# Context matmuls of the first expert layer: four column groups at a time, in rows of four sets, with gate and up weights alternating

## The chip, the cores and the metric

The kernel runs on one core of one Trainium2 chip. The metric is the device time of one execution in microseconds (us); the median of three runs before the change is 4630.0 us. The engines are named as the profile names them: PE (TensorE, the 128x128 array) with PEld (its weight loads), DVE (VectorE), ACT (ScalarE), POOL (GpSimd) and SP (SyncE, which issues the large transfers).

## The reference

The model is a trunk block followed by two layers of a second block. Only the last step of each of the two layers matters here, the mixture of experts in which every expert chooses its rows:

```python
def expert_choice_moe(h, w_router, w_gate, w_up, w_down):
    cap = EC_FACTOR * n // N_EXPERTS          # 128 of 1024 latent rows, 32 of 256 context rows
    aff = softmax(h @ w_router)
    g, idx = top_k(swapaxes(aff, 1, 2), cap)
    xs = h[idx]
    hid = silu(xs @ w_gate[e]) * (xs @ w_up[e])      # 1024 -> 512
    y = (hid @ w_down[e]) * g                        # 512 -> 1024
    return zeros.at[idx].add(y)
...
x = x + g2 * expert_choice_moe(modulate_2(x, sh2, sc2), ...)
if not last:                                  # the first of the two layers alone
    xc = xc + cg2 * expert_choice_moe(modulate_2(xc, csh2, csc2), ...)   # the same weights
```

All inputs are float32. There are 16 experts. In the first layer each expert works on 128 latent rows and on 32 context rows with the same weights; in the second layer on the latent rows alone.

## The kernel before

`Block2.experts` (from line 998) is called once a layer. **Weights** come in pieces of 512 KB, a tile `raw` of 128x1024 float32: `moe_plan` (line 900) lists them in the order of use. An expert has twelve: four of gate (two blocks of 128 features each), four of up, and, one expert later in the list, four of down. `fetch` issues their transfers on SP into `NR` rotating tiles; `moe_bufs` (line 146) gives `NR` = 13 for the first layer and 19 (and four early ones) for the second. `cut` splits each piece into a high and a low part, `wh` = the piece rounded to the fp32r type (a cast on ACT, line 1023) and `wl` = piece - `wh` (a subtraction on DVE, on POOL for every fourth piece, line 1024), into `NS` = 6 pairs of tiles, five pieces ahead of their use. `part` hands out the next pair.

**Latent rows.** `mm3` (lines 86 to 89) makes each product of the 128 rows of three fp32r matmuls with 512 moving columns (high x high, high x low, low x high). The way up has 8 such triples for gate (into PSUM tile `pg`) and 8 for up (`pu`), the way down 8 (`py0`, `py1`).

**Context rows.** Their 32 rows are multiplied in plain float32 straight with the unsplit piece, by `groups` (line 1059): the stationary operand has 32 columns, so it takes a fourth of the array's columns, and up to four different blocks of 256 weight columns can run in the four fourths. On the way up every `mm3` triple is followed by one *set* of two such matmuls: gate columns in fourths 0 and 1, up columns in fourths 2 and 3 of `pcx`. On the way down every two triples are followed by a set of four matmuls into `pcy`. In the trace each of these matmuls is two instructions. A `raw` tile can be loaded again only when its subtraction and its context matmuls are done.

**Order.** The instructions of this stage stand on each engine in the order of the program (`manual_schedule`). For expert e it is: way up of e; transposes of the next expert's gathered rows (line 1052); way down of e-1; transposes of the hidden rows (lines 1097 and 1102). After the way up, `th`, `hid` (lines 1080 to 1083) and their context twins `thc`, `upc`, `hcx` (lines 1086 to 1091) turn `pg`, `pu` and `pcx` into hidden rows; after the way down, `y` (line 1145) and `yc` (line 1125) weight the rows, and POOL's indirect DMAs add them to the rows they came from (lines 1146 and 1127). POOL also issues the gathers (line 1038). The last expert of the first layer has its four context sets of the way down ahead of its triples, four in a row.

Of the kernel before, what the change touches and what calls it, by code (L numbers as in the profile page):

```python
# [24 lines left out]
def bc_rows(ap, n, extra=()):  # L25
    """DRAM vector read by every partition."""
    return bass.AP(tensor=ap.tensor, offset=ap.offset, ap=[[0, P]] + list(extra) + [[1, n]])


class Base:  # L30
# [23 lines left out]
    def rsqrt(self, pool, ss, n, scale, eps, out=None):  # L54
        """(ss * scale + eps) ** -0.5 of a [128, n] tile, by Newton's iteration."""
# [6 lines left out]
        # every step turns the sign  # L62
# [28 lines left out]
    # adaptive modulation -------------------------------------------------  # L91
    def ada_new(self, pool, pre, w_ap, bcol_ap, brow_ap, cc_ap, gates):
        """A modulation to be worked out by chunks; gates: {chunk: DRAM rows [2, 512]}."""
# [18 lines left out]
    def ada_steps(self, m, ap, pp, chunks, nk=2, bufs=3, pb=1):  # L112
        """One chunk a step."""
# [29 lines left out]
class Block2(Base):  # L143
    NE = 16
    moe_early = (0, 4)
    moe_bufs = ((13, 6, 5), (19, 6, 5))
# [7 lines left out]
    def mods2(self, l, ap, pp, bufs=3):  # L154
        """The modulation of a layer, in steps: rows of shifts, 1 + scales and gates.
        Every fourth of the columns goes through its own fourth of the array."""
# [32 lines left out]
    def mod_row(self, pool, l, w, i, n=1, name="mr", q=None, **kw):  # L189
        """n modulation rows from the i-th on every partition."""  # L190
        t = pool.tile([P, n, 1024], F32, name=name, **kw)
        (q or self.nc.sync).dma_start(t, bass.AP(tensor=self.mrow.tensor, offset=self.mrow[w, l, 1024 * i:].offset, ap=[[0, P], [1, 1024 * n]]))
        return t

    def norm(self, srcs, A, B, sp, pp, sink, rows=None, between=None, xbufs=2, copy=None):
        """srcs: list of (dram [n,1024] or SBUF [128,T,1024], first tile, tiles, which); sink(k, tok0, n, f32 tile).
        between: run after the rows are scaled; copy: engine of each scaled copy of SBUF rows."""
# [39 lines left out]
    # ---------------------------------------------------------------------  # L237
    def layer(self, l, xin, cin, xmid, cmid, hn, hnc, ready=False, crows=None):
        """xmid, cmid: the rows after this layer; hn, hnc: room for modulated rows;
        ready: its modulation is worked out; crows: the context's modulated rows, if they are. the experts are chosen."""  # L240
# [13 lines left out]
    def mixers(self, l, last, lp, xin, cin, crows):  # L254
# [27 lines left out]
        # ---- the input projection, by tiles of tokens  # L282
        with self.pool(f"w{l}") as wp, self.pool(f"wps{l}", space=PSUM) as pp:
# [15 lines left out]
            def weights(c0, cn):  # L299
                """A step splits a piece; the second parts go where the pieces split before were loaded."""  # L300
# [19 lines left out]
            # rows are scaled two tiles ahead of their products, and transposed one ahead  # L320
# [40 lines left out]
        # ---- what attention keeps  # L361
        hp = s_mix.enter_context(self.pool(f"hd{l}"))
        tps = s_mix.enter_context(self.pool(f"tps{l}", space=PSUM))
        # the rotated shared part of the keys
# [24 lines left out]
        def prep(h, S):  # L389
            """The operands of one head, in steps."""  # L390
# [72 lines left out]
        # ---- attention, one head's operands ahead  # L463
        hb = s_mix.enter_context(self.pool(f"hb{l}"))
        sets.append(head_set(hb))
        with self.pool(f"at{l}") as ap, self.pool(f"atps{l}", space=PSUM) as pp:
# [4 lines left out]
            def scores(u):  # L471
                """Unnormalised probabilities of 128 queries."""
# [84 lines left out]
    def rope2(self, dst, g, tmp):  # L557
        """dst [128, 8, 64] <- rotated g; they may be the same."""
# [10 lines left out]
    def ctx_rows(self, pool):  # L569
        """The context's rows as the first layer's input projection takes them."""  # L570
# [8 lines left out]
    def rows_in(self, x, ab, wp, fast=False):  # L579
        """The norm and the modulation of one tile of tokens."""  # L580
# [9 lines left out]
    def turn_in(self, x, wp, pp):  # L590
        """Features on partitions, as two parts."""
# [9 lines left out]
    def project_in(self, t, only_kv, h, fin, wp, pp, W, cqh, cql, ckh, ckl, kr, sskr, f, u2, gv, ssv, qln, kvln):  # L601
        """One tile of tokens: the projection, and what follows it row by row; returns the last step, fin is the last tile's."""
# [49 lines left out]
    def spatial(self, l, last, TQ, f, u2, gv, ssv, sgun, bsg):  # L652
        """Spatial gating and Fourier mixing."""
        nc, ins = self.nc, self.ins
        with self.pool(f"g{l}", side="right") as cp, self.pool(f"gps{l}", space=PSUM) as pp:
            def piece(k, o, n):
                """Room for n tokens from o of the k-th features, and the way to their place."""
                t = cp.tile([P, 512], F32, name="cat", bufs=2)
                return t, lambda: nc.sync.dma_start(self.catd[k * P:k * P + P, o:o + n], t[:, :n])
# [14 lines left out]
            # Fourier: the tokens  # L674
# [30 lines left out]
            # the gate  # L705
# [7 lines left out]
            # Fourier: the features  # L713
# [45 lines left out]
    def project(self, l, last, xin, cin, xmid, cmid, hn, hnc, ep):  # L759
        """The output projection, the rows' second norm, and the choice of every expert's rows.  # L760
        Returns the steps of the choice that are left."""
# [5 lines left out]
        with self.pool(f"r{l}", side="right") as rp, self.pool(f"rps{l}", space=PSUM) as pp:  # L767
            with self.pool(f"o{l}") as op_:
                # all the weights are on their way before there is room for their parts
# [19 lines left out]
                def turn(U):  # L789
                    """The router's view of a tile, and its affinities with those of the tiles before it."""  # L790
# [13 lines left out]
                def cat(c):  # L804
                    """The features of a tile."""
# [4 lines left out]
                def router(mr):  # L810
                    """The router's weights with the norm's scales, and what its shifts add."""
# [90 lines left out]
    def moe_plan(self, l):  # L902
        ins, plan = self.ins, []
        wg, wu, wd = (ins[n][l] for n in ("w_gate_2", "w_up_2", "w_down_2"))
        for e in range(self.NE + 1):
            if e < self.NE:
                for w in (wg, wu):
                    v = w[e].rearrange("(k p) f -> p k f", p=P)
                    plan += [v[:, k:k + 2, :] for k in range(0, 8, 2)]
# [5 lines left out]
    def route(self, rp, pp, U, af, o, tag, bufs=2):  # L915
        """Affinities of two tiles of tokens, experts on partitions from o."""
# [29 lines left out]
    def choose(self, w, T, cap, rp, pp, ep, af, tag, bufs=2):  # L946
        """The cap tokens of largest affinity of every expert, and their affinities.
        Many tokens go in two halves, sorted beside each other: of the i-th of one and the i-th last of the other
        the larger one is among the cap largest of both."""
# [48 lines left out]
    def experts(self, l, last, xmid, cmid, hn, hnc, ep, af):  # L998
        """Every expert's rows, weighted and gated, added to the rows they came from."""
        nc, ins, idx, gt = self.nc, self.ins, self.idx, self.gt  # L1000
        NE = self.NE
        with self.pool(f"x{l}") as xp, self.pool(f"xps{l}", space=PSUM) as pp, self.tc.manual_schedule():
            # the weights in the order of their use, split some pieces ahead of it
# [55 lines left out]
            def groups(out, xc, w, j0, n, start, stop):  # L1059
                """Columns of w by fourths of the array; n of them from group j0."""  # L1060
                for g in range(n):
                    nc.tensor.matmul(out[32 * (j0 + g):32 * (j0 + g) + 32, :], xc, w[:, 256 * g:256 * g + 256],  # L1062
                                     start=start, stop=stop, tile_position=(0, 32 * (j0 + g)))

            def up(U):
# [4 lines left out]
                for mi, dst in enumerate((pg, pu)):  # L1070
                    for k0 in range(0, 8, 2):
                        w = part()
                        for j in range(2):
                            k = k0 + j
                            self.mm3(dst, xh[:, k], xl[:, k], w[0][:, j], w[1][:, j], k == 0, k == 7)
                            if not last:
                                c = slice(32 * (U["e"] % 4), 32 * (U["e"] % 4) + 32)
                                groups(pcx, U["xc"][:, k, c], w[2][:, j], 2 * mi, 2, k == 0, k == 7)
# [28 lines left out]
            def down(U):  # L1107
# [9 lines left out]
                def ctx(k, w):  # L1117
                    if not last:
                        groups(pcy, U["hct"][:, k], w[2].rearrange("p a b -> p (a b)"), 0, 4, k == 0, k == 3)
# [10 lines left out]
                if e == NE - 1 and not last:  # L1130
                    w = [part() for _ in range(4)]
                    for k in range(4):
                        ctx(k, w[k])
# [3 lines left out]
                else:  # L1137
                    for k in range(4):
                        w = part()
                        main(k, w)  # L1140
                        ctx(k, w)
# [21 lines left out]
            # rows are gathered two experts ahead; an expert's way down comes after the next one's way up  # L1163
# [1061 lines left out]
```

## Time and profile before

| | us |
|---|---|
| median of three runs | 4630.0 |
| lowest and highest | 4618.5, 4631.8 |
| span of the profiled execution | 4613.0 |
| of it: first layer's experts, from the first gate matmul to the last way down | about 3016 to 3561 |
| of it: second layer's experts, from the first gate matmul to the last row addition | about 4264 to 4603 |

| engine | busy us | share of the span |
|---|---|---|
| PE | 4229.6 | 92% |
| PEld | 3189.4 | 69% |
| DVE | 2803.5 | 61% |
| ACT | 1835.0 | 40% |
| POOL | 1057.6 | 23% |

The span runs from the first to the last instruction of one execution; the run's time has some us around it. [...] A matmul's recorded duration includes the pipeline behind it, so what one costs in a stream is the distance between two starts, not its duration.

### The profile page before, as it was taken

How to read it: one execution, taken by the hardware profiler on the slowest of the kernel's cores; microseconds unless marked ns; L12 is line 12 of the kernel's file. 1: busy time of each engine (PE TensorE's matmuls, PEld its weight loads, DVE VectorE, ACT ScalarE, POOL GpSimd, SP SyncE). 2: the span in 40 equal slices, each digit the busy share in tenths (PEclk: the TensorE clock that was granted, in tenths of full speed). 3: DMA queues.
4: the chain of work that ended last, by engine and by line, in shares of the span. 5: the costliest groups of instructions: out<-in, count | busy, mean ns of one | idle time of the engine just before them, and what ended most of it. 6: DMA issues, size and time to landing. Idle time of an engine off the chain costs nothing. (4 is left out here: it accounts for less than half of the span.)

```text
span 4613.0 us, 70037 instructions
## 1 busy us (share of the span) xinstructions
PE 4229.6 (92%) x27212; PEld 3189.4 (69%) x27212; DVE 2803.5 (61%) x5419; ACT 1835.0 (40%) x3590; POOL 1057.6 (23%) x863
## 2 busy tenths in 40 slices
PE   7998999999799999999897999889998889995988
PEld 6874567777667888889786777544444767774776
DVE  5365557677686544445655665655555656656888
ACT  4233234444433211212344664144443436641665
POOL 1000012222131201100211212433342202224564
PEclk9999989899999999999898999899999889997999
DMA  6226635555562322220302013467776110135996
GB/s 230 68 87 200 206 102 127 148 124 126 106 204 90 127 86 92 92 79 27 122 19 77 13 46 122 147 202 227 216 222 190 67 57 18 53 107 198 317 349 213
DMA packets 433204, 611.92 MB, mean 133 GB/s; under 512 B 93888, under 2 KB 259920, under 8 KB 431976
## 3 DMA queue, kind: packets, MB, share of 16 engines
q1 hardware_dynamic: 403800, 527.74, 35.8%
q0 software_dynamic: 29072, 79.70, 6.6%
q8 instruction: 214, 3.51, 0.3%
q14 instruction: 118, 0.97, 0.1%
HBM read 510.29 MB, written 97.05 MB: 132 GB/s over the span
## 5 line engine op out<-in xcount | busy, mean ns | idle before, releaser
L1024 DVE TENSOR_TENSOR wl<-raw,wh 128x1024 fp32r<-128x1024 f32 x284 | 402.6, 1464 | 129.3 <-ACT wh L1023 127.2
L1023 ACT CAST wh<-raw 128x1024 fp32r<-128x1024 f32 x384 | 390.0, 1052 | 184.3 <-PE pg L89 107.2
L1024 POOL TENSOR_TENSOR wl<-raw,wh 128x1024 fp32r<-128x1024 f32 x100 | 257.6, 2582 | 420.1 <-ACT wh L1023 382.2
L87 PE MATMUL pu<-z,uh 128*128 128x256 f32 x1024 | 293.7, 287 | 4.6 <-ACT uh L77 4.6
L89 PE MATMUL pu<-z,ul 128*128 128x256 f32 x1024 | 291.1, 284 | 2.3 <-DVE ul L78 2.3
L88 PE MATMUL pu<-hl,uh 128*128 128x256 f32 x1024 | 291.0, 284 | 0.0
L2057 DVE TENSOR_TENSOR x<-x,pd 128x512 f32<-128x512 f32 x256 | 174.3, 686 | 128.2 <-PE pd L89 128.2
L87 PE MATMUL gps<-wh,hh 128*128 128x512 f32 (+2 forms) x656 | 225.5, 344 | 18.1 <-ACT hh L77 13.1
L2029 POOL TENSOR_TENSOR raw<-raw,g 128x1024 f32<-128x1024 f32 x32 | 82.1, 2580 | 638.5 <-DMA raw<-w_mlp_down 455.3
L89 PE MATMUL gps<-wh,hl 128*128 128x512 f32 (+2 forms) x656 | 222.4, 340 | 1.2 <-POOL hl L1356 1.0
L87 PEld LDWEIGHTS pu<-z,uh 128*128 128x128 f32 x1024 | 197.6, 193 | 14.8 <-issue 5.3
L87 PE MATMUL pd<-dh,ah 128*128 128x512 f32 x512 | 200.1, 391 | 2.2 <-DVE x L2057 2.0
L88 PE MATMUL pd<-dl,ah 128*128 128x512 f32 x512 | 199.6, 390 | 0.0
L89 PE MATMUL pd<-dh,al 128*128 128x512 f32 x512 | 199.5, 390 | 0.0
L89 PEld LDWEIGHTS pu<-z,ul 128*128 128x128 f32 x1024 | 197.4, 193 | 2.6 <-DVE ul L78 2.6
L88 PEld LDWEIGHTS pu<-hl,uh 128*128 128x128 f32 x1024 | 197.6, 193 | 0.1
L1062 PE MATMUL pcx<-raw,xc 128*32 128x256 f32 x1024 | 160.4, 392 | 0.0
L77 ACT CAST wh<-raw 128x512 fp32r<-128x512 f32 (+1 forms) x120 | 73.5, 614 | 203.2 <-PE gp L88 85.7
L87 PEld LDWEIGHTS gps<-wh,hh 128*128 128x128 f32 x656 | 130.8, 200 | 32.2 <-ACT hh L77 14.3
L77 ACT CAST dh<-raw 128x1024 fp32r<-128x1024 f32 x32 | 32.2, 1048 | 282.3 <-PE pd L89 276.2
L89 PEld LDWEIGHTS gps<-wh,hl 128*128 128x128 f32 x656 | 130.7, 200 | 15.0 <-POOL hl L1356 1.5
L2046 DVE TENSOR_TENSOR r<-r 128x512 f32<-128x512 f32 x64 | 54.1, 845 | 142.2 <-ACT ah L2045 142.2
(676 smaller groups left out, 12226.7 us busy)
## 6 DMA issues: line engine op xcount, KB each, us to landing
araw<-w_ada SPq DMA_DIRECT2D x144, 512.0 KB
raw<-w_gate SPq DMA_DIRECT2D x128, 512.0 KB
raw<-w_up SPq DMA_DIRECT2D x128, 512.0 KB
raw<-w_down SPq DMA_DIRECT2D x128, 512.0 KB
raw<-w_in SPq DMA_DIRECT2D x100, 256.0 KB
raw<-w_mlp_up SPq DMA_DIRECT2D x32, 512.0 KB
raw<-w_mlp_down SPq DMA_DIRECT2D x32, 512.0 KB
x<-x SPq DMA_DIRECT2D x24, 512.0 KB
```

Of the source, the lines that this page charges most:

```text
L77: nc.scalar.copy(hi, src)
L87: mm(ps, lh, rh, start=start, stop=False)
L88: mm(ps, lh, rl, start=False, stop=False)
L89: mm(ps, ll, rh, start=False, stop=stop)
L1023: nc.scalar.copy(h, raw)
L1024: (nc.gpsimd if ahead or i % 4 == 3 else nc.vector).tensor_tensor(lo, raw, asf(h), op=OP.subtract)
L1062: nc.tensor.matmul(out[32 * (j0 + g):32 * (j0 + g) + 32, :], xc, w[:, 256 * g:256 * g + 256], start=start, stop=stop, tile_position=(0, 32 ...
L2029: nc.gpsimd.tensor_tensor(raw2, raw2, g2, op=OP.mult)
L2046: nc.vector.tensor_tensor(r, r, r, op=OP.mult)
L2057: nc.vector.tensor_tensor(x[:, t, s], x[:, t, s], p, op=OP.add)
```

## The change

Four edits, all in `moe_plan`, `moe_bufs` and `experts`. The plan lists gate and up pieces by turns (gate 0, up 0, gate 1, up 1, ...), in both layers. The way up takes one piece of each at a time: two triples into `pg`, two into `pu`. In the first layer its context matmuls are kept back until two such pairs of pieces are through, and then run as four sets in a row, each set of four matmuls (gate columns in fourths 0 and 1, up columns in 2 and 3 at the same time); this happens twice an expert. On the way down the four context sets come in a row after all triples. `NR` of the first layer is 18 instead of 13. The full diff also takes out comments and docstrings; nothing else differs.

```diff
-    moe_bufs = ((13, 6, 5), (19, 6, 5))
+    moe_bufs = ((18, 6, 5), (19, 6, 5))
...
-                for w in (wg, wu):
-                    v = w[e].rearrange("(k p) f -> p k f", p=P)
-                    plan += [v[:, k:k + 2, :] for k in range(0, 8, 2)]
+                vs = [w[e].rearrange("(k p) f -> p k f", p=P) for w in (wg, wu)]
+                plan += [v[:, k:k + 2, :] for k in range(0, 8, 2) for v in vs]
...
-            def groups(out, xc, w, j0, n, start, stop):
-                for g in range(n):
-                    nc.tensor.matmul(out[32 * (j0 + g):32 * (j0 + g) + 32, :], xc, w[:, 256 * g:256 * g + 256],
-                                     start=start, stop=stop, tile_position=(0, 32 * (j0 + g)))
+            def groups(out, sets, start=True, stop=True):
+                for i, (xc, ws) in enumerate(sets):
+                    for g in range(4):
+                        nc.tensor.matmul(out[32 * g:32 * g + 32, :], xc, ws[g], start=start and i == 0, stop=stop and i == len(sets) - 1,
+                                         tile_position=(0, 32 * g))
...
-                for mi, dst in enumerate((pg, pu)):
-                    for k0 in range(0, 8, 2):
-                        w = part()
+                sets, c = [], slice(32 * (U["e"] % 4), 32 * (U["e"] % 4) + 32)
+                for k0 in range(0, 8, 2):
+                    w2 = [part() for _ in range(2)]
+                    for w, dst in zip(w2, (pg, pu)):
                         for j in range(2):
-                            k = k0 + j
-                            self.mm3(dst, xh[:, k], xl[:, k], w[0][:, j], w[1][:, j], k == 0, k == 7)
-                            if not last:
-                                c = slice(32 * (U["e"] % 4), 32 * (U["e"] % 4) + 32)
-                                groups(pcx, U["xc"][:, k, c], w[2][:, j], 2 * mi, 2, k == 0, k == 7)
+                            self.mm3(dst, xh[:, k0 + j], xl[:, k0 + j], w[0][:, j], w[1][:, j], k0 + j == 0, k0 + j == 7)
+                    if not last:
+                        sets += [(U["xc"][:, k0 + j, c], [w[2][:, j, o:o + 256] for w in w2 for o in (0, 256)]) for j in range(2)]
+                        if len(sets) == 4:
+                            groups(pcx, sets, k0 == 4 - 2, k0 == 6)
+                            sets = []
...
-                def ctx(k, w):
+                def ctx(w):
                     if not last:
-                        groups(pcy, U["hct"][:, k], w[2].rearrange("p a b -> p (a b)"), 0, 4, k == 0, k == 3)
+                        groups(pcy, [(U["hct"][:, k], [w[k][2].rearrange("p a b -> p (a b)")[:, 256 * g:256 * g + 256] for g in range(4)]) for k in range(4)])
...
+                    w = []
                     for k in range(4):
-                        w = part()
-                        main(k, w)
-                        ctx(k, w)
+                        w.append(part())
+                        main(k, w[k])
+                    ctx(w)
```

## Rows read from the trace of the kernel before

**Rows 1.** The page, busy shares: busy time of PE, granted clock in 40 slices.

```profile
PE 4229.6 (92%) x27212; PEld 3189.4 (69%) x27212; DVE 2803.5 (61%) x5419; ACT 1835.0 (40%) x3590; POOL 1057.6 (23%) x863
...
PEclk9999989899999999999898999899999889997999
```

**Rows 2.** Windows: first layer's experts, second layer's; busy us by engine, clock, DMA.

```profile
core 0: us, PE busy (x) PEld busy (x) DVE busy (x) ACT busy (x) POOL busy (x), PEclk, DMA share, GB/s
...
3070.00:3200.00 130.00, 128.67 (x700) 62.42 (x698) 69.16 (x87) 57.20 (x69) 47.90 (x25) 1.00 0.76 227
...
4281.00:4601.00 320.00, 286.89 (x1267) 229.34 (x1266) 288.87 (x239) 209.37 (x237) 177.21 (x72) 0.96 0.90 304
```

**Rows 3.** Waits in the first layer's experts: total us, times, longest.

```profile
ACT wh L1023 <- PE pg L89: 91.3, 49, 2.2
...
PE tps L1052 <- DVE xl L78: 4.0, 3, 1.3
...
SPq L1015 <- PE pcx L1062: 322.6, 123, 9.9
```

**Rows 4.** Timeline of PE, one expert: start, length, line, tile, shape.

```profile
3179.72 0.50 PE L87 MATMUL pg<-wh,xh 128*128 128x512 f32 x1
...
3181.17 0.50 PE L87 MATMUL pg<-wh,xh 128*128 128x512 f32 x1
3181.50 0.39 PE L88 MATMUL pg<-wl,xh 128*128 128x512 f32 x1
3181.73 0.40 PE L89 MATMUL pg<-wh,xl 128*128 128x512 f32 x1
3182.06 0.62 PE L1062 MATMUL pcx<-raw,xc 128*32 128x256 f32 x4
3182.62 0.50 PE L87 MATMUL pg<-wh,xh 128*128 128x512 f32 x1
...
3202.87 1.10 PE L1052 MATMUL tps<-ident,xg 128*128 128x128 f32 x8
...
3205.30 0.64 PE L1062 MATMUL pcy<-raw,hct 128*32 128x256 f32 x8
3205.86 0.51 PE L87 MATMUL py<-wh,hdh 128*128 128x512 f32 x1
...
3213.22 0.50 PE L87 MATMUL pg<-wh,xh 128*128 128x512 f32 x1
```

**Rows 5.** Timeline of PE, last expert: four context sets in a row.

```profile
3554.73 1.93 PE L1062 MATMUL pcy<-raw,hct 128*32 128x256 f32 x32 [2.20 <-DVE hct L1104]
3556.60 0.51 PE L87 MATMUL py<-wh,hdh 128*128 128x512 f32 x1
```

**Rows 6.** Groups by line and shape, first layer's experts: busy us, mean ns.

```profile
L1024 DVE TENSOR_TENSOR wl<-raw,wh 128x1024 fp32r<-128x1024 f32 x139 | 165.1, 1223 | 122.5 <-ACT wh L1023 120.6 <-DMA raw<-w_up 1.7
...
L1024 POOL TENSOR_TENSOR wl<-raw,wh 128x1024 fp32r<-128x1024 f32 x47 | 117.8, 2507 | 323.2 <-ACT wh L1023 299.9 <-issue 23.3
...
L1062 PEld LDWEIGHTS pcx<-raw,xc 128*32 128x32 f32 x1016 | 36.7, 108 | 92.5 <-issue 92.5
```

**Rows 7.** The same for the second layer's experts, 4290 to 4550 us.

```profile
L1024 DVE TENSOR_TENSOR wl<-raw,wh 128x1024 fp32r<-128x1024 f32 x110 | 185.3, 1742 | 2.3 <-ACT wh L1023 2.2
```

**Rows 8.** Timelines of POOL and DVE, second layer: two row additions; splits beside each other.

```profile
4301.79 1.64 POOL L1146 DMA_INDIRECT out<-y,idx  x1 [3.82 <-ACT wh L1023]
...
4574.43 2.60 POOL L1146 DMA_INDIRECT out<-y,idx  x1 [0.16 <-ACT wh L1023]
...
4368.89 9.02 DVE L1024 TENSOR_TENSOR wl<-raw,wh 128x1024 fp32r<-128x1024 f32 x4
...
4369.84 5.85 POOL L1024 TENSOR_TENSOR wl<-raw,wh 128x1024 fp32r<-128x1024 f32 x2
```

**Rows 9.** Window before the first layer's experts, while the first pieces arrive.

```profile
2980.00:3000.00 20.00, 4.07 (x24) 1.54 (x22) 19.62 (x58) 2.31 (x5) 10.23 (x7) 0.51 1.02 383
```

**Rows 10.** Timeline of PE, the first expert's first matmuls, at half the clock.

```profile
3016.36 0.63 PE L88 MATMUL pg<-wl,xh 128*128 128x512 f32 x1
3016.78 0.63 PE L89 MATMUL pg<-wh,xl 128*128 128x512 f32 x1
```

More of the change, by code (lines that the diff above doesn't have):

```diff
@@ L1131, in down @@
                     w = [part() for _ in range(4)]
-                    for k in range(4):
-                        ctx(k, w[k])
+                    ctx(w)
                     out_ctx()
@@ L1137, in down @@
                 else:
+                    w = []
                     for k in range(4):
-                        w = part()
-                        main(k, w)
-                        ctx(k, w)
+                        w.append(part())
+                        main(k, w[k])
+                    ctx(w)
                 y = xp.tile([P, 1024], F32, name="y", bufs=2)
```

## The prediction

> **What bounds the kernel now.** I read the page's busy shares first: PE is busy for 92% of the span and its clock is nearly always granted [rows 1], so the kernel is a chain of stages that PE mostly fills, and each must be looked at by itself. The windows by stage come next. In the first layer's experts PE is busy 128.67 of 130 us at clock 1.00 while DVE has 69 and the DMA engines a share of 0.76; in the second layer's experts PE is busy 287 of 320 us, DVE 289 and DMA 0.90 [rows 2]. The two layers run the same loop with different bounds: the first is PE's alone, the second is shared by DVE and the transfers. The waits confirm it for the first layer: ACT waits for PE to free a split tile, SP waits for PE's context matmuls to free a `raw` tile, and PE's own longest wait there, but for the last expert's, is 1.3 us [rows 3]. Last comes the timeline of one expert: it takes 33.50 us from one first gate matmul to the next, 23.15 of it the way up [rows 4]. Every triple of three matmuls there is followed by a context set, and that set is what the change regroups.
>
> **What a context set costs now.** Two fp32r matmuls in a stream start 0.23 us apart (line 88 to 89). Round a set, line 89 to the next line 87 is 0.89 us, and that line 87 to line 88 takes 0.33 instead of 0.23 [rows 4]. So a set costs 0.89 - 0.23 + 0.10 = 0.76 us, of which only 0.56 lies between its first instruction and the next triple. Check: 23.15 - 48 x 0.23 = 12.11 us for 16 sets, 0.757 each. The way down has four sets of four groups, and one of them also takes 0.56 us (3205.30 to 3205.86) [rows 4]: **four fourths of the array cost what two cost**.
>
> **What a set costs in a row of four.** The last expert shows it: 32 instructions, four sets, take 3554.73 to 3556.60 = 1.87 us [rows 5]. Each set after the first adds (1.87 - 0.56) / 3 = 0.44 us, and the change between triples and sets is paid once. A row of four costs 0.76 + 3 x 0.44 = 2.07 us.
>
> **The change part by part.**
> *Way up*: 16 sets at 12.11 us become two rows of four, 4.14 us: 7.97 us less, for 16 experts 127.5 us. All of it is on PE's path, the path that sets the end.
> *Way down*: 4 x 0.76 = 3.04 becomes 2.07: 0.97 us less. The last expert has the row already, so 15 x 0.97 = 14.6 us. Sum 142.1 us; an expert goes to 33.50 - 8.94 = 24.56 us.
> *Gate and up by turns*: `pg` is now complete two triples (1.4 us) ahead of `pu` instead of half a way up, so `th` starts later. Its cover is the second row of sets, 2.07 us, then the transposes and the way down of the expert before; hidden rows are needed only after that. ACT stands 2.07 instead of 0.56 us behind `thc`, which waits for `pcx`, with the splits for the way down's last pieces behind it; five pieces are split ahead, about 7 us of triples, so nobody waits. I cost it at nothing; without that cover it would be about 1.5 us an expert, 24 us.
> *Second layer*: the order of its pieces changes, not their number, size or engine; `hid` still waits for the end of `pu`, and POOL still has every fourth piece. I take 0, between a loss and a gain of some us.
> *18 raw tiles*: up to four wait for a row of sets and five are split ahead, which leaves 9 to 13 on their way, against 7 now (13 less five split ahead and one in use); SP issues four transfers in a burst after each row instead of one at a time, and only weights are queued behind them there. At the entry 5 x 0.52 = 2.6 MB more are fetched, 6.8 us at the 383 GB/s of that time [rows 9], before the first gathers, and the two modulation rows that SP loads behind them come later; the first way down that needs those is 50 us off. Bounds 0 to 6.8 us once; I take 0, because the entry waits for the choice of the experts, which runs on DVE.
> *What is late next*: the transfers. An expert moves 227 GB/s x 33.50 = 7.6 MB. At the first layer's share that is 0.76 x 33.50 = 25.5 us of all DMA engines, at the second layer's rate per share (304 / 0.90 = 338 GB/s) 22.5 us [rows 2]. 22.5 us at that layer's share of 0.90 is a period of 25.0 us; against 24.56 it costs 0.4 us, 7 us in all. I take this end, since the second layer moves nearly the same pieces at the density that the first one would reach.
>
> The sum is 142 - 7 = 135 us off the profiled execution's span of 4613.0 us, 4478. The median of the runs lies 17.0 us above that span and the fastest run 5.5; I keep the 17: **4495 us**.
>
> **The rivals.**
> *The splits bind.* In the second layer DVE's split takes 1742 ns in the mean against 1223 in the first [rows 6, 7]: four of them take 9.02 us where POOL subtracts beside them for 5.85 us [rows 8]. A subtraction of DVE that starts while POOL's runs is held until POOL is through. The second layer's expert takes (4574.43 - 4301.79) / 13 = 21.0 us [rows 8], though PE needs 72 x 0.23 + 1.8 for transposes (33.50 - 23.15 - 24 x 0.23 - 3.04) = 18.4. The 2.6 us between, on 16 experts of the first layer, are 42 us: 4530 us. Against it: DVE needs 69.16 / 130 x 33.50 = 17.8 us an expert now [rows 2], with nine splits at 1742 ns 22.5, below 24.56. [...]
> *The transfers bind.* If packets keep the first layer's cost, 25.5 us of engines at a share of 0.90 make 28.3 us an expert: 3.7 x 16 = 60 us back, 4548 us. For it speaks that SP's transfers now come in bursts; against it the 383 GB/s at the entry [rows 9].
> *A set costs more in the way up.* If the weight loads of the sets that follow (108 ns, two a set [rows 6]) don't hide behind the matmuls before them, a row costs 3 x 2 x 0.108 = 0.65 us more, three rows and 16 experts 31 us: 4519 us without the 7 of the transfers. [...] The last expert's 0.44 us a set has no room for two exposed loads behind two streams of 256 float32 columns [rows 5], so the trace speaks against it. That the four groups run one after another, so that the change does not do what it says, is excluded by the equal 0.56 us.
> *Slower: the clock.* If PE, faster than its supply, waits so often in the first layer's experts that it is granted only 0.50, matmuls start 0.42 us apart as at the first expert's start [rows 10] and an expert takes about 24.56 x 0.42 / 0.23 = 44.8 us: 16 x 11.3 = 181 us lost, 4811 us. It decides from the point where more than (33.50 - 24.56) / (44.8 - 24.56) = 44% of the stage is at half the clock. Against it: the second layer's experts, where PE does wait, are granted 0.96 [rows 2].
>
> **How the numbers follow.** Forecast (4476 to 4512) 0.74; splits bind 0.10; transfers bind 0.08; sets cost more 0.05; clock 0.03. A measurement of this kernel tells about 0.3% (14 us) from no change. All but the last give more than that: faster 0.96, within 0.01, slower 0.03. The range begins at 4476, the full 142 us and the 12 us by which the fastest run lies below the median, and ends at 4535, behind the splits' and the sets' cases; transfers and clock are left out.
>
> **What would show it.** In the changed profile: two rows of 32 context instructions a way up, each some 1.9 us long; an expert's period of 24.5 to 25.0 us; PE busy over 97% in that stage at clock 1.00, DVE at 0.75 to 0.9, DMA share 0.9 at about 305 GB/s. DVE splits above 1.5 us in the mean with PE waiting for `wl` would show the first rival; ACT or DVE waiting for `raw` the second; sets more than 0.45 us apart the third. I am wrong if the second layer or the entry moves by more than 10 us, or if the period stays above 26 us.

## The result

The changed kernel takes 4476.3 us in the median of four runs (4472.5 to 4478.3), the kernel before 4626.6 in the four runs beside them (4618.5 to 4631.8): a ratio of 0.968, 95% interval 0.966 to 0.970. The profiled execution has a span of 4474.4 us, 138.6 less than the span of before. Lines stand one number lower than before (1023 is the subtraction, 1051 the transposes, 1022 the cast); `groups` stays at 1062.

The page, busy shares and granted clock in 40 slices, as [rows 1]:

```profile
PE 4087.1 (91%) x27212; PEld 3208.8 (72%) x27212; DVE 2825.1 (63%) x5419; ACT 1835.9 (41%) x3590; POOL 1066.3 (24%) x863
...
PEclk9999998899989999999999999989998989997999
```

The count of instructions on PE is the same, 27212, and PE is busy for 142.5 us less. The windows of the two expert stages, as [rows 2] (us, busy us of PE, PEld, DVE, ACT and POOL, clock, DMA share, GB/s):

```profile
3060.00:3330.00 270.00, 265.85 (x2000) 191.65 (x1990) 213.81 (x248) 162.85 (x201) 140.09 (x69) 1.00 0.91 306
...
4150.00:4430.00 280.00, 249.60 (x1099) 199.78 (x1098) 250.22 (x211) 185.15 (x209) 160.07 (x65) 0.95 0.96 328
```

In the first layer's experts PE is still the bound: 265.85 of 270 us, 98.5%, at clock 1.00. DVE's busy share has gone from 0.53 to 0.79 and the transfers from 227 to 306 GB/s, since the same work is done in less time. PE in one expert, as [rows 4]:

```profile
3137.41 0.50 PE L87 MATMUL pg<-wh,xh 128*128 128x512 f32 x1
3137.74 0.39 PE L88 MATMUL pg<-wl,xh 128*128 128x512 f32 x1
...
3143.08 1.93 PE L1062 MATMUL pcx<-raw,xc 128*32 128x256 f32 x32
...
3150.61 1.93 PE L1062 MATMUL pcx<-raw,xc 128*32 128x256 f32 x32
...
3152.47 1.09 PE L1051 MATMUL tps<-ident,xg 128*128 128x128 f32 x8
...
3158.99 1.93 PE L1062 MATMUL pcy<-raw,hct 128*32 128x256 f32 x32
...
3161.70 0.50 PE L87 MATMUL pg<-wh,xh 128*128 128x512 f32 x1
```

The way up takes 3152.47 - 3137.41 = 15.06 us against 23.15, the period 3161.70 - 3137.41 = 24.29 against 33.50. All experts but the first and every fourth repeat these figures; every fourth has a period of 26.9 us, and 36.0 before. The row at 3150.61 ends in 1.86 us, as the last expert's row did [rows 5]. DVE's and POOL's subtractions, first layer (3060 to 3330) and second (4150 to 4430), as [rows 6, 7]:

```profile
L1023 DVE TENSOR_TENSOR wl<-raw,wh 128x1024 fp32r<-128x1024 f32 x96 | 133.7, 1442 | 12.3 <-ACT wh L1022 12.3
...
L1023 POOL TENSOR_TENSOR wl<-raw,wh 128x1024 fp32r<-128x1024 f32 x33 | 87.1, 2639 | 123.3 <-ACT wh L1022 122.4 <-issue 0.6
...
L1023 DVE TENSOR_TENSOR wl<-raw,wh 128x1024 fp32r<-128x1024 f32 x120 | 196.5, 1695 | 3.1 <-ACT wh L1022 3.1
```

DVE's subtraction has become longer in the first layer, 1442 ns against 1223, but PE waits for none of the pieces' subtractions there, nor for `th` or `hid`. Two of the longest sums among the waits of that layer (3060 to 3400; us in total, times, longest), both of engines ahead of PE, as in [rows 3]:

```profile
POOL wl L1023 <- ACT wh L1022: 155.8, 28, 9.2
...
ACT wh L1022 <- PE pg L89: 35.7, 28, 2.4
```

**Where the time went, by stage.** From the first gate matmul of the first layer's experts to PE's next operation behind them it was 3572.88 - 3015.76 = 557.12 us before and is 3429.64 - 3018.87 = 410.77 now: 146.35 less. The way up gives 16 x 8.09 and the way down 15 x 1.13 (7.52 us against 8.65), together 146.4. That is the stage to within about 1 us: up to its last matmul it is 145.1 us shorter, and PE's next operation comes 1.3 us sooner behind that. The rest of the span gives back 7.7: the stage begins 3.1 us later, the stretch between the two layers' experts is 1.5 shorter, and the second layer's experts take 343.3 us from first gate matmul to last way down against 337.2, 6.1 more.

### The profile page after: what moved, and what is told of

It is laid out like the page before. It is cut to its first block, busy times and chain, and to the rows that moved or that the text cites. A ratio compares the mean times of both kernels' runs of the same rounds, so it can differ in the third digit from the quotient of the medians.

```text
span 4474.4 us, 70037 instructions
## 1 busy us (share of the span) xinstructions
PE 4087.1 (91%) x27212; PEld 3208.8 (72%) x27212; DVE 2825.1 (63%) x5419; ACT 1835.9 (41%) x3590; POOL 1066.3 (24%) x863
## 5 line engine op out<-in xcount | busy, mean ns | idle before, releaser
L1023 DVE TENSOR_TENSOR wl<-raw,wh 128x1024 fp32r<-128x1024 f32 x284 | 430.7, 1569 | 24.7 <-ACT wh L1022 24.4
L1022 ACT CAST wh<-raw 128x1024 fp32r<-128x1024 f32 x384 | 386.5, 1053 | 84.2 <-PE pg L89 52.3
L78 DVE TENSOR_TENSOR ptl<-tps,pth 128x512 fp32r<-128x512 f32 (+1 forms) x200 | 110.9, 588 | 42.6 <-ACT pth L77 41.5
```

The lines of the kernel that those rows point to most:

```text
L78: nc.vector.tensor_tensor(lo, src, asf(hi), op=OP.subtract)
L1022: nc.scalar.copy(h, raw)
L1023: (nc.gpsimd if ahead or i % 4 == 3 else nc.vector).tensor_tensor(lo, raw, asf(h), op=OP.subtract)
```

## The experiments

Each is an edit of the changed kernel, but for the first. A time without a range is a single run. "Stage" is the time from the first gate matmul to the last way down of a layer's experts: 546.2 us in the first layer before and 401.2 after the change, 337.2 and 343.3 in the second.

**The kernel before, profiled again.** No edit.

> The kernel before, once more, for a second profile. The changed kernel's span is 138.6 us below the span of the profile of before, but its median is 150.3 us below the median of before: the profile of before may have been a quick one. If so, this span lies between 4613 and 4630 us, the first layer's experts still take 33.5 us each, and the extra us stand in some other stage; if the span is 4613 again, time outside the span is what differs.

The span is 4615.5 us and the run 4617.3; first stage 546.05, second 339.7. The stage that the change touches repeats within 0.2 us, the second layer's within 2.5. A run is 1.8 us above its own span, here as in the changed kernel (4476.18 and 4474.4). In all, 27 timed runs of before lie between 4614 and 4639, and both profiled executions at the low end of that.

**Thirteen raw tiles.**

```diff
-    moe_bufs = ((18, 6, 5), (19, 6, 5))
+    moe_bufs = ((13, 6, 5), (19, 6, 5))
```

> The changed kernel with 13 raw tiles as before, all else as changed. Nine pieces are held or split ahead at the end of a row's wait, so four to eight are on their way. If transfers have room (my forecast), a piece still comes some 8 us after its tile is freed and is wanted 8 to 14 us after it: period of an expert 24.3 to 25 us, time 4476 to 4490 us. If the transfers are close to binding, PE or the engines that split wait for raw pieces: period 26 us or more, time above 4500 us.

Measured 4474.0 us in the median of four (4472.0 to 4478.4), first stage 400.0. The window of the first stage is the same to a hundredth of PE's time:

```profile
3060.00:3330.00 270.00, 265.86 (x2006) 191.28 (x2005) 213.82 (x248) 161.71 (x199) 141.11 (x69) 1.00 0.92 305
```

So thirteen tiles carry the new order, and the five more are neither needed nor paid for: the stage begins at 3019.6 us here and at 3018.9 with eighteen, so the larger prefetch at the entry cost nothing either.

**Four fourths, but each set alone.** The sets of four fourths are kept, and each follows its pair of triples; on the way down too each set stands alone (not shown):

```diff
+    for j in range(2):
+        for w, dst in zip(w2, (pg, pu)):
+            self.mm3(dst, ..., w[0][:, j], w[1][:, j], k0 + j == 0, k0 + j == 7)
+        groups(pcx, [(U["xc"][:, k0 + j, c], [...])], k0 + j == 0, k0 + j == 7)
```

> The changed kernel with the rows of four taken apart: four fourths at a time and gate and up by turns as changed, but each context set stands alone between triples (8 a way up, 4 a way down). By my prices a set alone costs 0.76 us and one in a row 0.44 after the first: way up 8 x 0.76 - 4.14 = 1.9 us longer, way down 1.0 longer, 16 x 1.9 + 15 x 1.0 = 46 us, time about 4522 us. If the loads of a row's later sets did not hide, the difference would be smaller, about 15 us.

Measured 4532.9, first stage 453.4. PE's timeline:

```profile
3128.39 0.40 PE L89 MATMUL pu<-wh,xl 128*128 128x512 f32 x1
3128.72 0.64 PE L1062 MATMUL pcx<-raw,xc 128*32 128x256 f32 x8
3129.29 0.50 PE L87 MATMUL pg<-wh,xh 128*128 128x512 f32 x1
...
3130.89 0.64 PE L1062 MATMUL pcx<-raw,xc 128*32 128x256 f32 x8
```

Eight instructions take 3129.29 - 3128.72 = 0.57 us, as four did before. The way up is 17.33 us. The 48 matmuls of a second-layer way up that waits for nothing take 11.02, so a set alone costs (17.33 - 11.02) / 8 = 0.79 us and one in a row of four (15.06 - 11.02) / 8 = 0.505. This splits the gain of the way up: filling the fourths is worth 23.15 - 17.33 = 5.8 us an expert, standing in rows 17.33 - 15.06 = 2.3. With about 1.1 of the way down the rows make 3.3 us an expert, and the stage moved by 52.3 / 16 = 3.3.

**Rows of four by halves of the array.** Same matmuls, first the four sets in fourths 0 and 1, then the four in 2 and 3:

```diff
+    for gs in ((0, 1), (2, 3)):
         for i, (xc, ws) in enumerate(sets):
-            for g in range(4):
+            for g in gs:
```

> The changed kernel with the packing taken apart: the same rows, but each row runs its four sets first in fourths 0 and 1 and then in fourths 2 and 3, so two matmuls at a time instead of four, eight half sets in a row. If four fourths cost what two cost, each row is longer by 4 x 0.44 = 1.75 us: three rows, 5.3 us an expert, 16 x 5.3 = 84 us, time about 4560 us. If the groups of a set ran one after another, nothing would change: 4476 us.

Measured 4528.5, first stage 443.6: 42.4 us more than the changed kernel, about half of what I had expected.

```profile
3136.43 2.82 PE L1063 MATMUL pcx<-raw,xc 128*32 128x256 f32 x32
3139.19 0.50 PE L87 MATMUL pg<-wh,xh 128*128 128x512 f32 x1
```

A row takes 3139.19 - 3136.43 = 2.76 us, not twice 1.87. Worked back from the row's end, 3139.19 - 1.87, the second half starts at about 3137.3, when fourths 0 and 1 are in the fifth of their eight passes (0.22 us each). From 3137.30 to 3137.36 six matmuls of the row run at once, where two fourths alone have four, each 0.38 us long. So the fourths fill the array, as the change says, and two of them need not run in step with the other two. Why the second half starts in the fifth pass and not earlier stays open.

**One set of each row.** This kernel leaves out three of the four context sets of every row, so its context rows are not what the reference computes.

```diff
-    groups(pcx, sets, k0 == 4 - 2, k0 == 6)
+    groups(pcx, sets[:1], k0 == 4 - 2, k0 == 6)
...
-    groups(pcy, [... for k in range(4)])
+    groups(pcy, [... for k in range(1)])
```

> The changed kernel, leaving out three of the four context sets of every row (the context rows are then not what the reference has); triples, splits, transfers and the number of held raw tiles stay. It asks what is late next. A row of four costs 2.02 us in the trace of the changed kernel (way up 15.06 = 11.02 + 2 rows), a set alone about 0.75: three rows give 3.8 us, so if PE still binds the period goes from 24.3 to 20.5 us and the time to about 4415 us. If the splits on DVE and POOL or the transfers bind at the 22.5 us that I worked out for each, the period stays near 22.5 and the time near 4447 us.

Measured 4446.4, first stage 360.3: 40.9 us less, 2.55 an expert, where three rows of three sets fewer would be 3 x (1.87 - 0.57) = 3.9. That mean hides two kinds of expert. Of the fifteen periods seven are 20.4 us and two, of every fourth expert, 23.05, which is 3.9 us below the changed kernel's 24.29 and 26.9: there PE still binds, at what the expectation had for that case. Five others take 21.5 to 28.0 us, and the loss stands in them. So there is no even next bound at 24.29 - 2.55 = 21.7 or at 22.5 us, and that the time came to within 1 us of the second case's 4447 is an accident: this execution's first gate matmul came 13.4 us later than the changed kernel's, and its second layer took 6.1 us less. The windows and two of the waits of that stage:

```profile
3060.00:3200.00 140.00, 130.37 (x693) 95.65 (x691) 127.20 (x144) 91.98 (x115) 89.20 (x39) 0.98 0.99 334
3200.00:3330.00 130.00, 126.04 (x674) 93.29 (x674) 117.54 (x132) 90.20 (x111) 84.54 (x37) 0.99 1.02 340
```

```profile
PEld pu L88 <- POOL wl L1023: 8.4, 4, 3.0
PEld tps L1051 <- DVE xl L78: 8.0, 5, 4.4
```

PE drops to 130.37 of 140 us, and what it waits for are the subtractions of POOL and DVE (`xl` is the low part of the gathered rows). The transfers are at 334 to 340 GB/s and a share of 0.99 to 1.02 at the same time, but in these two windows ACT's casts wait for a piece 0.7 us in all, so the splits end last there and not the transfers.

**The second layer in its old order.** Gate, then up, for the second layer alone; the first keeps the change.

```diff
-    plan += [v[:, k:k + 2, :] for k in range(0, 8, 2) for v in vs]
+    plan += [v[:, k:k + 2, :] for v in vs for k in range(0, 8, 2)] if l == 1 else [...]
```

> The changed kernel with the second layer's pieces and triples in the order of before (all gate, then all up). The second layer's experts took 337 and 340 us in two profiles of before and 340 to 343.5 in four of the changed order; three or four of its gathers take 6.1 us on POOL instead of 1 to 2, with four such in the 343 us ones. If the order is the cause: three long gathers and 337 to 340 us here, 3 to 6 us less than the changed kernel. If chance: 340 to 344 us.

Measured 4478.3 (4475.6 to 4483.4), second stage 341.05 with four gathers of about 6 us. This does not bring back the 337.2. With the old order (before, before again and this kernel) the second stage took 337.2 to 341.1 us, with the new one (the changed kernel, the four experiments above and the next one) 337.2 to 343.5: the order is not shown to cost anything.

What does go with the length is the count of long gathers. The profiles with three of them (before, before again, thirteen tiles, one set of each row) have 337.2 to 340.2 us, those with four (the changed kernel, the sets alone, the halves and this one) 341.1 to 343.5. POOL's subtraction of a piece stands behind the gather, and in all of these profiles each long gather is followed, some 8.5 us after its start, by a wait of PE of 2.8 to 4.4 us for that subtraction. Here the first of the changed kernel, on POOL and on PE:

```profile
4179.24 6.10 POOL L1037 DMA_INDIRECT xg<-hn,idx  x1 [0.30 <-issue]
4185.37 4.66 POOL L1023 TENSOR_TENSOR wl<-raw,wh 128x1024 fp32r<-128x1024 f32 x2
```

```profile
4187.77 0.79 PE L88 MATMUL pu<-wl,xh 128*128 128x512 f32 x1 [4.40 <-POOL wl L1023]
...
4188.78 0.63 PE L87 MATMUL pu<-wh,xh 128*128 128x512 f32 x1
4189.21 0.63 PE L88 MATMUL pu<-wl,xh 128*128 128x512 f32 x1
```

Behind the wait PE is granted 0.50, half of its 1.00, from 4188 to 4193 us, and its matmuls start 0.43 us apart instead of 0.23.

**The second layer's gather earlier.** POOL issues the gather of expert e + 2 behind the way up of e instead of ahead of it.

> The changed kernel with the second layer's gather issued right after the way up instead of after the way down, so that POOL runs it while DVE works from PSUM. In the trace the 6.1 us gathers lie beside four or five subtractions of DVE back to back and end when DVE turns to an operation from PSUM. [...] If the long gathers wait for their transfers' queue, nothing changes: 4476 us.

The second layer's gathers in the changed kernel and in this one (ns: shortest, median, longest), then DVE's subtractions and PE's wait for them in this one (4150 to 4430):

```profile
L1037 POOL DMA_INDIRECT xg<-hn,idx x12: 1105/1546/6099, 4158.9 to 4394.6; - x12
```

```profile
L1037 POOL DMA_INDIRECT xg<-hn,idx x13: 985/1789/1794, 4149.6 to 4406.5; - x13
...
L1023 DVE TENSOR_TENSOR wl<-raw,wh 128x1024 fp32r<-128x1024 f32 x118 | 223.2, 1951 | 0.7 <-ACT wh L1022 0.6
...
L88 PE MATMUL pu<-wl,xh 128*128 128x512 f32 x104 | 43.6, 419 | 32.9 <-DVE wl L1023 32.9
```

The long gathers are gone, and the second stage takes 343.2 us, as before the edit; timed 4488.5 (4480.0 to 4499.2), not faster. This profile is of the quickest of the four runs. PE's waits for POOL's subtraction are gone with the long gathers, but what PE waits for instead is DVE's subtraction, now 1951 ns in the mean. So my theory that short gathers alone would free the second layer, which I had put at 12 us and 4464 us, falls.

**All subtractions of the second layer on DVE.**

```diff
-    (nc.gpsimd if ahead or i % 4 == 3 else nc.vector).tensor_tensor(lo, raw, asf(h), op=OP.subtract)
+    (nc.gpsimd if ahead or (i % 4 == 3 and not last) else nc.vector).tensor_tensor(lo, raw, asf(h), op=OP.subtract)
```

> The changed kernel with all subtractions of the second layer's pieces on DVE, none on POOL. If the splits there are slow because DVE's subtraction is held while POOL's runs (1742 ns in the mean against 1216 alone), DVE needs 12 x 1.22 + 5 = 19.6 us an expert and the period falls from 21.0 to about 19.8: 20 us less, 4456 us. If DVE is short of time anyway, three more subtractions an expert cost 3.6 us each expert: 4530 us.

Measured 4433.1 us (4431.3 to 4439.1), a ratio to before of 0.959 (0.956 to 0.962). The second stage falls from 343.3 to 295.0 us, though DVE has a third more subtractions to do.

```profile
4140.00:4400.00 260.00, 259.00 (x1215) 212.69 (x1214) 258.38 (x272) 202.86 (x233) 122.54 (x26) 1.00 1.02 370
...
L1023 DVE TENSOR_TENSOR wl<-raw,wh 128x1024 fp32r<-128x1024 f32 x174 | 199.8, 1216 | 0.3 <-ACT wh L1022 0.3
...
L1037 POOL DMA_INDIRECT xg<-hn,idx x12: 8317/8368/8385, 4159.2 to 4358.6; - x12
...
4302.55 9.16 DVE L1023 TENSOR_TENSOR wl<-raw,wh 128x1024 fp32r<-128x1024 f32 x8
```

And the changed kernel's DVE and POOL in the same layer:

```profile
4311.18 7.58 DVE L1023 TENSOR_TENSOR wl<-raw,wh 128x1024 fp32r<-128x1024 f32 x3 [0.24 <-ACT wh L1022]
```

```profile
4310.68 2.54 POOL L1023 TENSOR_TENSOR wl<-raw,wh 128x1024 fp32r<-128x1024 f32 x1
...
4315.16 2.52 POOL L1023 TENSOR_TENSOR wl<-raw,wh 128x1024 fp32r<-128x1024 f32 x1 [1.95 <-ACT wh L1022]
```

Beside POOL's two subtractions three of DVE's take 7.58 us; without POOL eight take 9.16. In the single instructions the two that run into one of POOL's take 3.11 and 3.41 us and end 1.08 us after POOL's end, and the one between them takes 1.21. PE is busy 259.00 of 260 us with all of them on DVE: the second layer is PE's as well, with periods of 17.7 to 18.2 us behind the first expert, where the changed kernel's go from 17.7 to 26.8.

The edit takes more away than DVE's held subtractions. The whole second stage, of the changed kernel and of this one, and PE's waits for subtractions in that stage of the changed kernel; in this one it has none:

```profile
4119.20:4463.00 343.80, 306.02 (x1338) 244.66 (x1336) 301.68 (x252) 221.90 (x250) 185.42 (x75) 0.95 0.87 294
```

```profile
4122.60:4418.00 295.40, 290.19 (x1337) 237.01 (x1336) 283.14 (x298) 218.67 (x250) 124.09 (x27) 0.98 0.96 342
```

```profile
PE pu L88 <- POOL wl L1023: 16.6, 8, 4.4
...
PE pg L88 <- DVE wl L1023: 7.1, 5, 1.9
...
PE pu L88 <- DVE wl L1023: 6.8, 6, 2.0
...
PE py L88 <- DVE wl L1023: 2.0, 4, 0.5
```

PE waited 16.6 us for POOL's own subtractions, 15.9 for DVE's, and was busy 15.8 us longer with the same matmuls, at a granted clock of 0.95 against 0.98. Together these three are the 48.3 us to within about 1 us. No run parts what POOL's subtraction costs by holding DVE from what it costs by coming late itself.

**Rows of eight, on top of the last edit.**

```diff
-    if len(sets) == 4:
-        groups(pcx, sets, k0 == 4 - 2, k0 == 6)
+    if len(sets) == 8:
+        groups(pcx, sets)
```

> The kernel of e8 (the second layer's subtractions all on DVE) with one row of eight context sets a way up instead of two of four; 18 raw tiles. A set alone costs 0.79 us in e3 and each further one of a row 0.41, so a row of eight costs 3.66 us against 4.04: 0.38 us an expert, 6 us in all, 4427 us against 4433. Eight pieces wait for the row and five are split ahead, which leaves five on their way at the least, one more than 13 tiles left with rows of four, which cost nothing. If the burst of eight transfers comes too late, PE or the splits wait for raw pieces and the gain is gone: 4433 us or more.

```profile
3124.57 3.66 PE L1062 MATMUL pcx<-raw,xc 128*32 128x256 f32 x64
3128.16 1.09 PE L1051 MATMUL tps<-ident,xg 128*128 128x128 f32 x8
```

The way up takes 14.70 us, 0.36 less, and the first stage 395.8, 5.6 less than with rows of four beside the same second layer (401.4). Timed it is 4431.9 (4426.5 to 4438.0), which the spread of the runs does not part from 4433.1. It gives a check of the set's price: with a for the change from triples to sets and back and b for a set, a + b = 0.79 and a + 4b = (15.06 - 11.02) / 2 = 2.02 give b = 0.41 and a = 0.38; a + 8b is 3.66, and the row of eight costs 14.70 - 11.02 = 3.68.

**All subtractions of both layers on DVE**, rows of four.

> The kernel of e8 with the first layer's subtractions too all on DVE. In the changed kernel PE binds that layer's experts (24.3 us each), and DVE's subtractions take 1442 ns in the mean there, 1216 without POOL: 12 x 1.22 + 7 = 21.6 us an expert, still below 24.3. If PE binds, nothing changes: 4433 us, with no wait of PE for a split. If DVE becomes the bound in bursts, the first layer's experts take longer than 401 us, some 0.5 us an expert: 4441 us.

Measured 4427.4 (4422.5 to 4446.1), first stage 401.2: nothing moves in the first layer, where PE has no room to be faster, and no wait of PE for a piece's split is in the profile.

```profile
3060.00:3330.00 270.00, 265.86 (x2002) 191.20 (x2000) 229.72 (x281) 161.71 (x197) 51.21 (x36) 1.00 0.91 305
```

The last three kernels beat both that this study began with, the changed one by 43 to 49 us; among themselves their runs don't part them.

## Why the prediction was right, and which of its terms was not

**The bound.** PE bounded the first layer's experts before and still does; a share of 98.5% at clock 1.00 was forecast as over 97%. A rival that puts the bound elsewhere has no place in that stage.

**The price of a set.** Forecast were 0.76 us for a set among triples, 0.44 more for each that follows in a row, 2.07 for a row of four, and 127.5 + 14.6 us in all. Measured are 2.02 for the row and 129.4 + 17.0 us. Of the four us between, the 32 rows of the ways up give about two (32 x 0.05 to 0.06) and the ways down the rest: 7.52 us each where 8.65 - 0.97 = 7.68 was forecast. The sets alone and the row of eight show the two parts of the price by themselves, a change of 0.38 us and 0.41 for each set.

**Gate and up by turns, 18 raw tiles, the entry.** All were costed at nothing. PE waits for none of `th`, `hid` and the pieces' splits, and thirteen tiles do as well as eighteen, entry included. The stage began 3.1 us later than in the profile of before, but the changed kernel and those of its variants that have the same code up to there reach the first gather's transposes anywhere from 3013 to 3029 us, and the two profiles of before at 3011 and 3013; no row ties this to the change.

**The transfers.** This is the first term that was mis-sized. I took 7 us for a period of 25.0 instead of 24.56, because in the second layer a share of 0.90 stood beside a PE that waited. It does not mean that transfers bind there: this stage runs at 0.91 without a wait for them of more than 0.4 us, and the second layer went on to 1.02 and 370 GB/s once the subtractions were moved. The right allowance was 0, and with it and the cheaper rows the period came to 24.29, below the 24.5 to 25.0 that was to show the forecast.

**The second layer.** Costed at 0, bounds some us on either side; in the profiles it is 6.1 us longer. The order of its pieces is not shown to explain that, and with the new order it lies between 337 and 344. The difference of the two profiles is one more long gather, four instead of three, with the wait for POOL's subtraction behind it: PE waits 16.6 us for those in the stage instead of 11.9, and some of its matmuls behind the wait run at half the clock (0.50). Why one execution has three and another four stays open. Timed, the kernels differ by 4626.6 - 4476.3 = 150.3 us, by the interval of the ratio 141 to 156, more than the 146.4 of the first stage alone, so the medians speak against a steady loss of 6 us. The prediction's 21.0 us an expert was a mean too, of experts that take 17.7 to 26.8 us.

**From span to median.** This is the larger mis-sized term. I kept 17 us for what the median lies above the profiled span, as if it lay around every execution. Around one there are 1.8 us; the other 15 are the difference between a quick execution, which the profile of before was, and the median of before. The profile of the changed kernel sits at its median. By spans the account of 4495 - 4476.3 = 18.7 us is 15.1 from this term, 7.0 from the transfers, 4.3 from the sets, less 7.7 that the rest of the span gave back. By medians it is 3.5 from the median of before (4630.0, then 4626.6 with one run more), 7.0 and 4.3 as above, and 4 that lie in no stage which the profiles could name.

**What was luck.** The mechanism and the stage's saving were right to 3% (142.1 forecast, 146.4 measured). The time was not: 4476.3 lies 18.7 us below the forecast and 0.3 us above the lower end of the range, 4476, which stood there because 12 us of spread between the fastest run and the median had been allowed. All the sizes that were off pointed the same way but those of the second layer and the entry; a little more of any of them would have put the time outside.

**The rivals.** *The splits bind* did not happen in the first layer: DVE's mean rose to 1442 ns, but 0.79 of its time was enough. Its mechanism shows in the trace, though (3.11 and 3.41 us for two subtractions that run into POOL's, 1.21 for the one between them), and the second layer is where it decides: 48 us there, 3.0 an expert, more than the 2.6 that the prediction had worked out from 21.0 less 18.4. The 18.4 is what PE needs there in the end (17.7 to 18.2), but the mechanism named only what DVE loses; the waits for POOL's own subtractions and the half clock behind them were not in it. *The transfers bind* falls by the thirteen tiles and by the 370 GB/s. *A set costs more in the way up* falls by 0.41 us a set, which is no more than in the last expert's row. *The clock* stayed at 1.00 in the stage.

## What to carry to other kernels

Where small matmuls stand among large ones, price three things apart from the timeline: the change between the two kinds (0.38 us here), a set in a row (0.41) and how many of the array's fourths a set leaves empty; here the empty fourths were worth 5.8 us an expert and the changes 3.3. A busy share of 0.9 of the transfers, or a wait that names a queue, does not yet make them the bound: look at what else holds the engine that waits, and take the suspect away. Before a mean saving is read as a new bound, look at the single periods: in the kernel with one set of each row most experts were still PE's. And don't add the distance between a median and one profiled span to a forecast as if it were a fixed cost; compare medians with medians and say how far one execution may stand from them.

## What the runs showed of the hardware

**In the second layer POOL's subtractions cost more than they saved.** The mean DVE subtraction was 1695 ns with POOL doing every fourth, and 1216 ns with POOL doing none; the layer went from 343.3 to 295.0 us. The expectation had put this at some 20 us. Not all of it is DVE's: 16.6 us were waits of PE for POOL's subtractions and 15.8 a slower PE. In the first layer, where PE binds, the same move changed nothing (401.4 and 401.2 us). In the single instructions of the changed kernel's second layer 33 of the 34 DVE subtractions that start while one of POOL's runs end 1.08 to 1.09 us after POOL's end and take 2.2 to 3.7 us; those beside none of POOL's take 1.21 in the median. In the profile of before it is 34 of 35, with the same 1.08 to 1.09 us. What holds them is not shown.

**Two halves of the array overlap.** From 0.87 us into a row by halves six of its matmuls ran at once, where two fourths alone have four, and the row took 2.76 us and not 3.74.

**Weight loads hide within a row.** In the single instructions of the row at 3143.08 the load for a fourth's next matmul starts, from the second pass on, 1 to 2 ns after that fourth's running matmul, takes 110 ns, and the next matmul starts 216 ns after the one before; two such passes are a set's 0.41 to 0.43 us. The last expert's row of the kernel before [rows 5] has the same: 1 to 3 ns, 109 to 111 and 215 to 216.

**The long gathers cost by what stood behind them on POOL.** With all subtractions of the second layer on DVE, which was busy 258.38 of 260 us, the gathers took 8.3 to 8.4 us each, where those of the changed kernel took 1.1 to 1.8 and four of them 6.1. The layer still took only 295.0 us, with no subtraction of POOL behind them. In the changed kernel a gather of 6.1 us was followed each time by a wait of PE of 2.8 to 4.4 us for POOL's subtraction.
